# A hybrid attention and convolution block on one core: how the down projection's plain weights and its y tiles are brought in

## The chip, the core and the metric

The kernel runs on one core of a Trainium2 chip. A core has a matmul engine (TensorE, PE in the profile), three engines that work on tiles (VectorE is DVE, ScalarE is ACT, GpSimd is POOL), a sync engine (SP) and DMA queues that SP, ACT and POOL issue to. An engine takes its instructions in the order in which they stand in its queue; an instruction that waits holds up all behind it. The metric is the device time of one execution in microseconds. The inputs are float32, one sequence of 512 tokens of width 2048.

## The reference

One layer: a mixer (neighbourhood attention beside a conformer convolution, gated and merged) and then a feed-forward block, each behind an RMS norm and added to the stream. What the change touches is the end of the second:

```python
h = h + rms_norm(swiglu(rms_norm(h, ffn_pre_g)) @ w_down, ffn_post_g)
# swiglu(u): silu(u @ w_gate) * (u @ w_up), of width 5632
# rms_norm(y, g): y * rsqrt(mean(y * y) + 1e-6) * g
```

The down projection takes 5632 = 44 x 128 activations to 2048 = 16 x 128 outputs, for 512 tokens.

## The kernel before

Everything is held transposed: a tile is 128 features by 512 tokens. Float32 products are made from split operands: `x` is cast to `xh` (the name of the type is fp32r) on ACT, and DVE makes `xl = x - xh`; a product is then three matmuls, hi x lo, hi x hi and lo x hi. For most of the work Strassen-like products take fewer matmuls (`strassen`); what is left are plain tiles.

The down projection runs over 44 tiles of activations in five stages:

- *First plain stage*, `products_and_operands(0, 0, False)`: activations 0 to 3 against all 16 outputs. Each output `o` takes 12 matmuls of 512 columns into `pd0_o`. Its weights, 128 x 512, are loaded on SP's queue (`raw_wd`), cast on ACT (`whi_wd`, L134) and subtracted on DVE (`wlo_wd`, L135). ACT then copies the result to a tile `yf` of three buffers (L897) and stores it in `y_d` in DRAM from its own queue (L901). After every second output `prepare` makes operands for the next stage: loads `da` on GpSimd's queue, sums `dt` on DVE (L203 to L206), casts on ACT (L157) and subtractions on DVE (L158).
- *First Strassen stage*, `pairs(0, ...)`: 16 activation tiles by seven products for each two outputs. The results `ys` are multiplied by a row on GpSimd and accumulated into `y_d` by GpSimd's DMA (`added`, L912 and L913).
- *Second plain stage*, `products_and_operands(1, 36, True)`: activations 36 to 39. It is as the first, except that `yf` is accumulated into `y_d` by GpSimd's DMA (L899).
- *Second Strassen stage*, `pairs(1, ...)`.
- *Last part*: activations 40 to 43. `half(0)` does 256 of the 512 tokens for all outputs, two outputs in one bank `pl`, and `half(1)` the others. In the first half `weights(o)` loads and splits the weights of two outputs (`wl`, L144) and loads their `y` from `y_d` on SP's queue. When a bank is full, DVE adds `y` (L981), ACT squares the sum (`ysq`, L982), DVE sums the squares (L992, L994, and L988 for the last pair). The column sums of the squares (`r_s`), their power on GpSimd (`r_r`) and its spread over the partitions (`r_b`) give the norm's factor. The first half's outputs are finished during the second half (L1018, L1022); the second half's behind its end: a multiplication `yg` on DVE (L1031), an addition of `hb` (L1034, three on GpSimd and five on DVE) and the store.

The order on each engine is made by a scheduler from the program's order and its estimates; `keep_in_program_order` fixes an instruction in its place. Tiles of 128 x 512 come from 66 buffers (`slot`), weights in the rough from five (`raw`), split weights of the plain stages from three each (`whi`, `wlo`), PSUM has four `bank` and four `abank`.

Of the kernel before, what the change touches and what calls it, by code (L numbers as in the profile page):

```python
# [27 lines left out]
AF = mybir.ActivationFunctionType  # L28
# [3 lines left out]
P = 128  # L32
# [30 lines left out]
EARLY = 3  # L63
UN_EARLY, YA_EARLY = 2, 3
# [5 lines left out]
def hybrid_block(ctx: ExitStack, tc, xT, vecs, rpb, mask, w_c0, w_qk, w_v, w_gg, w_cg, w_ao, w_co, w_out, w_g0, w_gu, w_dn, outT):  # L70
# [795 lines left out]


    def products_and_operands(n, k0, add):
# [23 lines left out]
        added()  # L892
        for o in range(KT):
            ps = (bank, abank)[o % 2](f"pd{n}_{o}")
            gemm([(ps, w_dn[o, :, k0 * P : (k0 + DN_P) * P])], acts, f"wd{n}_{o}", n=DN_P, pin=o < 2)
# [40 lines left out]
    acts.extend([load(DN_3 + k) for k in range(EARLY, DN_P)])  # L936
    added()
    ha = []
# [9 lines left out]
    w, y, yg, r4 = [], [], [], []  # L948

    def weights(o):  # L950

        raw = wraw(f"wl{o}").rearrange("p (n k) -> p n k", n=2)
        nc.sync.dma_start(raw, w_dn[o : o + 2, :, DN_3 * P :].rearrange("n p k -> p n k"))
        for i in range(2):
            w.append(split(raw[:, i], f"wl{o + i}"))
            y.append(slot(f"y{o + i}"))
            load_in_order(y[o + i], y_d[o + i])

    def half(n, between={}):

        cols, other = ((A, B), (B, A))[n]
        acc = None
        for o in range(0, KT, 2):
            if n == 0:
                weights(o)
            ps = (bank, abank)[o // 2 % 2](f"pl{n}_{o}")
            sq = slot(f"ysq{n}_{o}")
            for i, part in enumerate((other, cols)):
                hi, lo = w[o + i]
                for k in range(DN_P):  # L970
                    s = slice(k * P, (k + 1) * P)
                    ah, al = (t[:, cols] for t in acts[k])
                    for wt, t in ((hi, al), (hi, ah), (lo, ah)):
                        nc.tensor.matmul(
                            ps[:, part], wt[:, s], t, start=k == 0 and t is al, stop=k == DN_P - 1 and wt is lo,
                            skip_group_check=True,
                        )
            between.get(o, lambda: None)()
            for i, part in enumerate((other, cols)):
                t = y[o + i][:, cols]  # L980
                nc.vector.tensor_tensor(out=t, in0=ps[:, part], in1=t, op=ALU.add)  # L981
                nc.scalar.activation(sq[:, part], t, AF.Square)  # L982
# [4 lines left out]
                if o == KT - 2 and i == 0:  # L987
                    nc.vector.tensor_tensor(out=acc[:, cols], in0=acc[:, cols], in1=sq[:, other], op=ALU.add)  # L988
            if acc is None:
                acc = sq  # L990
            elif o < KT - 2:
                nc.vector.tensor_tensor(out=acc, in0=acc, in1=sq, op=ALU.add)  # L992
# [129 lines left out]
```

## Time and profile before

| what | us |
|---|---|
| median of 3 runs | 2573.63 (2569.06 to 2574.58) |
| the profiled execution | 2566.05 |
| its span in the trace | 2564.3 |
| PE busy | 2509.8 |
| DVE busy | 2010.9 |
| ACT busy | 1196.8 |
| POOL busy | 466.9 |
| first plain stage begins | 2056.87 |
| second plain stage begins | 2265.82 |
| last part begins | 2476.34 |

The profile is of one execution. Its rows give the start in us from the span's start, the busy time, the engine, the line, the operation and what it makes from what, then partitions x elements; "x8" means that eight like instructions are put together. In brackets stands how long the engine sat idle before, and what ended that. "PEclk" is the clock that PE was granted, as a share of full speed. A matmul's busy time overlaps that of the next, so the pace of matmuls is read from their starts. A row with "q" behind an engine's name is of its DMA queue.

### The profile page before, as it was taken

Reading aid. Unit: us, or ns where it says so; the run is one execution under the profiler, and the core shown is the slowest. Engines: PE = TensorE matmul, PEld = TensorE weight load, DVE = VectorE, ACT = ScalarE, POOL = GpSimd, SP = SyncE. Lnnn points to the kernel's source line nnn. Section 1 sums busy time; section 2 is a strip of 40 time slices with the busy share of each in tenths; the row PEclk is TensorE's granted clock in tenths of the full one; section 3 lists DMA queues with packets and bytes.
Section 4 is the critical chain, followed back from the end, with each engine's and each line's share of the span. In section 5 each row is a group of like instructions: output and inputs, shape, how many; then the busy total and the mean of one; then the engine's idle time right before and its main releaser. Section 6 shows DMA issues by size and latency. Waiting matters only on the chain. (4 is left out here: it accounts for less than half of the span.)

```text
span 2564.3 us, 35709 instructions
## 1 busy us (share of the span) xinstructions
PE 2509.8 (98%) x13407; PEld 2165.6 (84%) x13407; DVE 2010.9 (78%) x2602; ACT 1196.8 (47%) x1838; POOL 466.9 (18%) x504
## 2 busy tenths in 40 slices
PE   9999999999999999999999999999999999999986
PEld 8888888878888888888988888888888878878876
DVE  5999896677776654338898888899987889888866
ACT  5223333455555422225455555555555564465433
POOL 0110222210000021001101111222222125442332
PEclk9999999999999999999999999999999999999988
DMA  6246323576667445337255566667666678888772
GB/s 209 94 145 197 109 93 108 160 244 184 183 194 250 141 139 185 99 100 221 94 174 170 172 178 182 183 196 208 207 202 189 191 269 227 230 197 224 196 221 92
DMA packets 154636, 452.41 MB, mean 176 GB/s; under 512 B 18144, under 2 KB 25440, under 8 KB 154464
## 3 DMA queue, kind: packets, MB, share of 16 engines
q1 hardware_dynamic: 103456, 324.32, 37.6%
q0 software_dynamic: 30336, 90.20, 16.7%
q10 hardware_dynamic: 20672, 35.63, 3.8%
q8 instruction: 105, 1.72, 0.3%
q14 instruction: 67, 0.55, 0.1%
HBM read 381.39 MB, written 61.87 MB: 173 GB/s over the span
## 5 line engine op out<-in xcount | busy, mean ns | idle before, releaser
L410 DVE SCALAR_TENSOR_TENSOR cv<-z,vec,cv 128x497 f32<-128x497 f32 (+14 forms) x240 | 190.9, 797 | 4.8
L135 DVE TENSOR_TENSOR wlo_wo<-raw_wo,whi_wo 128x1024 fp32r<-128x1024 f32 x36 | 47.5, 1318 | 106.6 <-ACT whi_wo L134 106.1
L800 POOL TENSOR_TENSOR row<-row,asq 128x512 f32<-128x512 f32 x30 | 41.1, 1370 | 414.3 <-ACT asq L799 414.3
L134 ACT CAST whi_wo<-raw_wo 128x1024 fp32r<-128x1024 f32 x36 | 37.9, 1053 | 130.0 <-PE po L184 122.7
L912 POOL TENSOR_TENSOR ys<-ys,row 128x512 f32<-128x512 f32 x32 | 55.6, 1739 | 138.0 <-DVE ys L302 83.8
L134 ACT CAST whi_y<-raw_y 128x1024 fp32r<-128x1024 f32 x32 | 33.5, 1052 | 79.0 <-PE py L184 75.7
L134 ACT CAST whi_qk<-raw_qk 128x1024 fp32r<-128x1024 f32 x32 | 33.6, 1051 | 77.2 <-PE qk L184 56.5
L135 DVE TENSOR_TENSOR wlo_qk<-raw_qk,whi_qk 128x1024 fp32r<-128x1024 f32 x32 | 40.3, 1259 | 32.3 <-ACT whi_qk L134 32.1
L827 POOL TENSOR_TENSOR an<-an,row 128x512 f32<-128x512 f32 x32 | 51.2, 1603 | 69.2 <-DMA an<-a_d 45.7
L667 DVE TENSOR_TENSOR gg<-py,gg 128x512 f32<-128x512 f32 x32 | 21.8, 689 | 52.2 <-PE py L185 52.2
L135 DVE TENSOR_TENSOR wlo_y<-raw_y,whi_y 128x1024 fp32r<-128x1024 f32 x32 | 53.3, 1667 | 10.9 <-ACT whi_y L134 10.4
L322 POOL TENSOR_TENSOR r_r<-r_v,mhalf 128x2 f32<-128x2 f32 (+1 forms) x6 | 7.0, 1172 | 292.1 <-DVE r_v L320 241.8
L181 PE MATMUL py<-ycl,whi_y 128*128 128x512 f32 x128 | 49.8, 389 | 0.0
L184 PE MATMUL py<-ych,whi_y 128*128 128x512 f32 x128 | 49.8, 389 | 0.0
L185 PE MATMUL py<-ych,wlo_y 128*128 128x512 f32 x128 | 49.8, 389 | 0.0
L860 ACT ACTIVATE sg<-sg 128x512 f32<-128x512 f32 x39 | 24.7, 634 | 51.2 <-DVE sg L302 51.2
L491 POOL TENSOR_TENSOR bm<-braw,msk 128x128 f32<-128x128 f32 x56 | 41.3, 770 | 16.2 <-DMA braw<-in_rpb 16.2
L677 POOL TENSOR_TENSOR gg<-gg,gg 128x512 f32<-128x512 f32 x16 | 20.6, 1288 | 112.2 <-ACT whi_y L134 70.8
L418 POOL TENSOR_TENSOR csum<-csum,cv 128x512 f32<-128x512 f32 x7 | 12.7, 1820 | 144.4 <-DVE cv L410 144.4
L163 PE MATMUL f<-b,whi_f 128*128 128x256 f32 x128 | 36.5, 285 | 0.8 <-DVE b L158 0.8
L164 PE MATMUL f<-b,whi_f 128*128 128x256 f32 x128 | 36.3, 283 | 0.0
L165 PE MATMUL f<-b,wlo_f 128*128 128x256 f32 x128 | 36.3, 283 | 0.0
(3195 smaller groups left out, 8778.0 us busy)
## 6 DMA issues: line engine op xcount, KB each, us to landing
raw_wo<-in_w_out SPq DMA_DIRECT2D x36, 512.0 KB, 3.8
raw_qk<-in_w_qk SPq DMA_DIRECT2D x32, 512.0 KB, 3.8
a_d<-sg ACTq DMA_DIRECT2D x44, 256.0 KB, 3.7
raw_v<-in_w_v SPq DMA_DIRECT2D x16, 512.0 KB, 4.4
raw_y<-in_w_ao SPq DMA_DIRECT2D x16, 512.0 KB, 3.7
gg<-g_d SPq DMA_DIRECT2D x32, 256.0 KB, 4.4
raw_y<-in_w_co SPq DMA_DIRECT2D x16, 512.0 KB, 3.6
raw_f<-in_w_g SPq DMA_DIRECT2D x16, 512.0 KB, 3.4
```

The costliest lines, as they stand in the source:

```text
L134: cast(hi[:, s], raw[:, s])
L135: nc.vector.tensor_tensor(out=lo[:, s], in0=raw[:, s], in1=hi[:, s].bitcast(F32), op=ALU.subtract)
L163: nc.tensor.matmul(o, hi, t[:, B], start=first, stop=False, skip_group_check=True)
L164: nc.tensor.matmul(o, hi, t[:, A], start=False, stop=False, skip_group_check=True)
L181: mmul = nc.tensor.matmul(ps, hi[:, s], al, start=first, stop=False)
L184: nc.tensor.matmul(ps, hi[:, s], ah, start=False, stop=False)
L185: nc.tensor.matmul(ps, lo[:, s], ah, start=False, stop=last)
L410: nc.vector.scalar_tensor_tensor(out=a[:, to], in0=z[:, fr], scalar=col(C_WDW, i * CW + w), in1=a[:, to], op0=ALU.mult, op1=ALU.add)
L491: nc.gpsimd.tensor_tensor(out=bm[:, o + i - i0], in0=raw[:, :, i * BC : (i + 1) * BC], in1=msk[:, o + i - i0, None, :].broadcast_to([P, RO ...
L800: nc.gpsimd.tensor_tensor(out=row[n], in0=row[n], in1=sq, op=ALU.add)
L827: nc.gpsimd.tensor_tensor(out=t, in0=t, in1=row[k // KT], op=ALU.mult)
L912: tc.keep_in_program_order(nc.gpsimd.tensor_tensor(out=t, in0=t, in1=row[n], op=ALU.mult))
```

## The change

In both plain stages the weights of two outputs are loaded at once (`loaded`), cast in one instruction of 128 x 1024 and subtracted in one, and this stands in the program one pair ahead of the pair that uses it. `four` issues a tile's 12 matmuls. In the last part the weights of six outputs are issued ahead of the first, and each turn issues those six ahead (`kept`, `AHEAD`). The loads of `y` move from SP's queue to GpSimd's, 14 of them ahead of the last two accumulations and two behind these. The last pair's squares get a tile each and go to the column sums as they are, without DVE's addition (L988), so that these take six matmuls and not four. Of the eight last additions of `hb` four, not three, are GpSimd's.

```diff
--- before.py
+++ after.py
@@ -61,6 +61,7 @@
 S1_AT = 3
 SPLIT = 2
 EARLY = 3
+AHEAD = 6
 UN_EARLY, YA_EARLY = 2, 3
 C_PRE, C_POST, C_FPRE, C_FPOST, C_LNG, C_LNB, C_BDW, C_WDW = 0, 16, 32, 48, 64, 72, 80, 88
 C_N = C_WDW + CT * CW
@@ -864,6 +865,30 @@
         activated(j, t)
     left = list(range(FT - DN_A[0] - KT - 2, 2 * KT))
 
+    def loaded(o, k0):
+
+        raw = wraw(f"w{k0}_{o}")
+        nc.sync.dma_start(
+            raw.rearrange("p (n k) -> p n k", n=2), w_dn[o : o + 2, :, k0 * P : (k0 + DN_P) * P].rearrange("n p k -> p n k")
+        )
+        return raw
+
+    def weights(o, k0):
+        raw = loaded(o, k0)
+        return wchunk(raw, f"wd{k0}_{o}", raw=raw)
+
+    def four(ps, hi, lo, cols, pin=False):
+
+        for k in range(DN_P):
+            s = slice(k * P, (k + 1) * P)
+            ah, al = (t[:, cols] for t in acts[k])
+            for i, (wt, t) in enumerate(((hi, al), (hi, ah), (lo, ah))):
+                mmul = nc.tensor.matmul(
+                    ps, wt[:, s], t, start=k + i == 0, stop=k + i == DN_P + 1, skip_group_check=True
+                )
+                if pin and k + i == 0:
+                    tc.keep_in_program_order(mmul)
+
 
     def products_and_operands(n, k0, add):
 
@@ -890,9 +915,13 @@
         for c in range(2):
             load_rows(c)
         added()
+        w = [weights(0, k0)]
         for o in range(KT):
             ps = (bank, abank)[o % 2](f"pd{n}_{o}")
-            gemm([(ps, w_dn[o, :, k0 * P : (k0 + DN_P) * P])], acts, f"wd{n}_{o}", n=DN_P, pin=o < 2)
+            if o % 2 == 0 and o + 2 < KT:
+                w.append(weights(o + 2, k0))
+            hi, lo = (t[:, o % 2 * NT : (o % 2 + 1) * NT] for t in w[o // 2])
+            four(ps, hi, lo, slice(0, NT), pin=o < 2)
             t = stp.tile([P, NT], F32, tag="quad", name=f"yf{o}", bufs=3)
             nc.scalar.copy(t, ps)
             if add:
@@ -934,7 +963,12 @@
 
 
     acts.extend([load(DN_3 + k) for k in range(EARLY, DN_P)])
+    y = [slot(f"y{o}") for o in range(KT)]
+    for o in range(KT - 2):
+        tc.keep_in_program_order(nc.gpsimd.dma_start(y[o], y_d[o]))
     added()
+    for o in (KT - 2, KT - 1):
+        tc.keep_in_program_order(nc.gpsimd.dma_start(y[o], y_d[o]))
     ha = []
     for i in range(0, KT - 4, 4):
         t = stp.tile([P, 4, HN], F32, tag="S" if i else "S1", name=f"ha{i}")
@@ -945,54 +979,43 @@
         tc.keep_in_program_order(nc.gpsimd.dma_start(t, h_d[i : i + 2, :, A].rearrange("k p t -> p k t")))
         ha.extend((t[:, 0], t[:, 1]))
 
-    w, y, yg, r4 = [], [], [], []
-
-    def weights(o):
-
-        raw = wraw(f"wl{o}").rearrange("p (n k) -> p n k", n=2)
-        nc.sync.dma_start(raw, w_dn[o : o + 2, :, DN_3 * P :].rearrange("n p k -> p n k"))
-        for i in range(2):
-            w.append(split(raw[:, i], f"wl{o + i}"))
-            y.append(slot(f"y{o + i}"))
-            load_in_order(y[o + i], y_d[o + i])
+    w, yg, r4 = [], [], []
+
+    def kept(o):
+
+        raw = loaded(o, DN_3)
+        w.extend(split(raw[:, i * NT : (i + 1) * NT], f"wl{o + i}") for i in range(2))
 
     def half(n, between={}):
 
         cols, other = ((A, B), (B, A))[n]
-        acc = None
+        acc, last = None, []
+        if n == 0:
+            for o in range(0, AHEAD, 2):
+                kept(o)
         for o in range(0, KT, 2):
-            if n == 0:
-                weights(o)
+            if n == 0 and o + AHEAD < KT:
+                kept(o + AHEAD)
             ps = (bank, abank)[o // 2 % 2](f"pl{n}_{o}")
-            sq = slot(f"ysq{n}_{o}")
             for i, part in enumerate((other, cols)):
-                hi, lo = w[o + i]
-                for k in range(DN_P):
-                    s = slice(k * P, (k + 1) * P)
-                    ah, al = (t[:, cols] for t in acts[k])
-                    for wt, t in ((hi, al), (hi, ah), (lo, ah)):
-                        nc.tensor.matmul(
-                            ps[:, part], wt[:, s], t, start=k == 0 and t is al, stop=k == DN_P - 1 and wt is lo,
-                            skip_group_check=True,
-                        )
+                four(ps[:, part], *w[o + i], cols)
             between.get(o, lambda: None)()
+            sq = [slot(f"ysq{n}_{o}")] * 2 if o < KT - 2 else [slot(f"ysq{n}_{o + i}") for i in range(2)]
             for i, part in enumerate((other, cols)):
                 t = y[o + i][:, cols]
                 nc.vector.tensor_tensor(out=t, in0=ps[:, part], in1=t, op=ALU.add)
-                nc.scalar.activation(sq[:, part], t, AF.Square)
+                nc.scalar.activation(sq[i][:, part if o < KT - 2 else cols], t, AF.Square)
                 if n:
                     if (o + i) % 4 == 0:
                         yg.append(wp.tile([P, 4, HN], F32, tag="raw", name=f"yg{o}", bufs=5))
                     nc.scalar.activation(yg[-1][:, (o + i) % 4], t, AF.Copy, scale=col(C_FPOST, o + i))
-                if o == KT - 2 and i == 0:
-                    nc.vector.tensor_tensor(out=acc[:, cols], in0=acc[:, cols], in1=sq[:, other], op=ALU.add)
-            if acc is None:
-                acc = sq
+            if o == 0:
+                acc = sq[0]
             elif o < KT - 2:
-                nc.vector.tensor_tensor(out=acc, in0=acc, in1=sq, op=ALU.add)
+                nc.vector.tensor_tensor(out=acc, in0=acc, in1=sq[0], op=ALU.add)
             if o == KT - 4:
                 nc.vector.tensor_tensor(out=acc[:, cols], in0=acc[:, cols], in1=acc[:, other], op=ALU.add)
-        return acc, sq
+        return acc, *sq
 
     def halved(n, squares, pin=False):
 
@@ -1030,7 +1053,7 @@
         t = yg[g]
         nc.vector.tensor_tensor(out=t, in0=t, in1=rb, op=ALU.mult)
         for m in range(0, 4, 2):
-            e = nc.gpsimd if g == 0 or g == 2 and m == 0 else nc.vector
+            e = nc.gpsimd if g == 0 or g < 3 and m else nc.vector
             e.tensor_tensor(out=t[:, m : m + 2], in0=t[:, m : m + 2], in1=hb[g][:, m : m + 2], op=ALU.add)
             q = nc.scalar if m else nc.sync
             q.dma_start(ov[4 * g + m : 4 * g + m + 2, :, B].rearrange("k p t -> p k t"), t[:, m : m + 2])
```

ACT's queue in the first plain stage, where the copy of tile 3 stands (`yf3`; `pd0_3` is its bank, `d..._` are operands for the Strassen stage). Before, with the cast of tile 4 behind the copy:

```order
L897 COPY yf3_18534<-pd0_3_18515 128x512
L134 CAST whi_wd0_4_0_0_18539<-raw_wd0_4_0_0_18538 128x512
L901 DMA y_d_11000<-yf3_18534 128x512
L157 CAST d11_2_18563<-da2_0_18411 128x256
L157 CAST d22_0_18566<-da2_1_18412 128x256
L157 CAST d22_1_18569<-da2_1_18412 128x256
L157 CAST d122_0_18577<-dt2_18572 128x256
L157 CAST d122_1_18580<-dt2_18572 128x256
L157 CAST d342_0_18583<-dt2_18572 128x256
L157 CAST d342_1_18586<-dt2_18572 128x256
L134 CAST whi_wd0_5_0_0_18591<-raw_wd0_5_0_0_18590 128x512
L134 CAST whi_wd0_6_0_0_18613<-raw_wd0_6_0_0_18612 128x512
```

The same place after the change, where the pairs 0, 2 and 4 are cast ahead of `yf0`:

```order
L926 COPY yf3_18528<-pd0_3_18515 128x512
L135 CAST whi_wd0_6_18534<-raw_w0_6_18532 128x1024
L930 DMA y_d_11000<-yf3_18528 128x512
L926 COPY yf4_18550<-pd0_4_18531 128x512
L158 CAST d11_2_18557<-da2_0_18417 128x256
```

The weights of tiles 4 and 5 no longer stand behind `yf3`; those of 6 and 7 do.

ACT's queue at the end of the second plain stage (`d1_0h` are casts for the first Strassen products: `q` for the first of them, `s2` for the second, `s1` for the third). Before:

```order
L259 CAST d1_0h_21121<-d1_0q_21113 128x1024
L897 COPY yf13_21034<-pd1_13_21015 128x512
L157 CAST d347_1_21082<-dt7_21068 128x256
L897 COPY yf14_21056<-pd1_14_21037 128x512
L259 CAST d1_0h_21145<-d1_0s2_21141 128x1024
L259 CAST d1_0h_21165<-d1_0s1_21110 128x1024
L897 COPY yf15_21104<-pd1_15_21085 128x512
L259 CAST d1_0h_21190<-d1_0s3_21188 128x1024
```

After the change:

```order
L158 CAST d347_0_20989<-dt7_20978 128x256
L926 COPY yf14_20966<-pd1_14_20953 128x512
L158 CAST d347_1_20992<-dt7_20978 128x256
L926 COPY yf15_21008<-pd1_15_20995 128x512
L260 CAST d1_0h_21049<-d1_0s2_21045 128x1024
L260 CAST d1_0h_21069<-d1_0s1_21014 128x1024
```

The casts of `s2` and `s1` stood between the copies of tiles 14 and 15 and now stand behind both.

ACT's queue at the start of the last part (`wl4h` is the cast of output 4's weights, `ysq0_0` the squares of outputs 0 and 1). Before:

```order
L144 CAST fa43h_22595<-ad43_22593 128x512
L144 CAST wl0h_22615<-raw_wl0_22613 128x512
L144 CAST wl1h_22621<-raw_wl0_22613 128x512
L982 ACTIVATE ysq0_0_22628<-y0_22619 128x256
L144 CAST wl2h_22659<-raw_wl2_22657 128x512
L982 ACTIVATE ysq0_0_22628<-y1_22625 128x256
L144 CAST wl3h_22665<-raw_wl2_22657 128x512
L982 ACTIVATE ysq0_2_22672<-y2_22663 128x256
```

After the change:

```order
L145 CAST fa43h_22499<-ad43_22497 128x512
L145 CAST wl0h_22551<-raw_w40_0_22549 128x512
L145 CAST wl1h_22555<-raw_w40_0_22549 128x512
L145 CAST wl2h_22561<-raw_w40_2_22559 128x512
L145 CAST wl3h_22565<-raw_w40_2_22559 128x512
L145 CAST wl4h_22571<-raw_w40_4_22569 128x512
L145 CAST wl5h_22575<-raw_w40_4_22569 128x512
L145 CAST wl6h_22581<-raw_w40_6_22579 128x512
L145 CAST wl7h_22585<-raw_w40_6_22579 128x512
L1007 ACTIVATE ysq0_0_22614<-y0_22503 128x256
L145 CAST wl8h_22621<-raw_w40_8_22619 128x512
```

The casts of outputs 2 to 7 stood behind squares and now stand ahead of all of them. In DVE's queue the subtractions move with their casts.

## The prediction

> **What bounds the kernel now.** I read first the page's line of busy times, then the windows by stage, and then the timeline of the matmul engine (PE) around its gaps, with what ended each. Times are us from the span's start.
>
> ```profile
> PE 2509.8 (98%) x13407; PEld 2165.6 (84%) x13407; DVE 2010.9 (78%) x2602; ACT 1196.8 (47%) x1838; POOL 466.9 (18%) x504
> ...
> core 0: us, PE busy (x) PEld busy (x) DVE busy (x) ACT busy (x) POOL busy (x), PEclk, DMA share, GB/s
> 2060.00:2115.00 55.00, 50.36 (x216) 40.67 (x215) 49.94 (x110) 39.45 (x91) 9.12 (x14) 0.94 0.77 270
> 2115.00:2262.00 147.00, 147.00 (x845) 129.46 (x844) 131.69 (x131) 73.82 (x101) 69.95 (x68) 1.00 0.82 220
> 2262.00:2330.00 68.00, 62.52 (x287) 51.22 (x286) 56.77 (x119) 44.54 (x101) 26.03 (x33) 0.95 0.89 235
> ...
> 2470.00:2510.00 40.00, 27.23 (x151) 24.27 (x149) 15.88 (x30) 10.70 (x25) 8.03 (x9) 0.83 0.83 274
> ```
>
> PE is busy 98% of the span, and all of it in the Strassen stages (second window: 147.00 of 147.00 at clock 1.00). The change touches the stages where PE is not full: the two plain stages (50.36 of 55 and 62.52 of 68) and the last part (27.23 of 40, clock 0.83). What ends the gaps there, as the rows below show, is a cast of weights (tiles whi_wd, wl). So I price each stage by the end of its PE work; the next one starts there.
>
> **First plain stage.**
>
> ```profile
> 2056.87 0.40 PE L181 MATMUL pd<-fa0l,whi_wd 128*128 128x512 f32 x1
> ...
> 2070.96 0.50 PE L181 MATMUL pd<-fa0l,whi_wd 128*128 128x512 f32 x1 [3.02 <-ACT whi_wd L134]
> ...
> 2105.87 0.39 PE L181 MATMUL pd<-fa0l,whi_wd 128*128 128x512 f32 x1
> ...
> 2108.36 0.39 PE L185 MATMUL pd<-fa3h,wlo_wd 128*128 128x512 f32 x1
> ...
> 2069.80 0.58 ACT L897 COPY yf<-pd 128x512 f32<-128x512 f32 x1 [0.81 <-DMA y_d<-yf]
> 2070.28 0.62 ACT L134 CAST whi_wd<-raw_wd 128x512 fp32r<-128x512 f32 x1
> ...
> 2074.00:2076.00 2.00, 2.00 (x6) 1.63 (x5) 2.00 (x7) 1.00 (x4) 0.00 (x0) 0.50 0.45 132
> ```
>
> The last tile's first and last matmuls are 2105.87 and 2108.36, 11 steps of 0.226. A tile of 12 is 2.72, 16 tiles 43.5. The stage lasts 2108.36 + 0.23 − 2056.87 = 51.7, so 8.2 are lost. The loss begins with the fourth yf copy (2069.80), which waits until an earlier yf has landed (three buffers); the weight cast stands behind it in ACT's queue (2070.28) and PE sits 3.02. Then the clock falls to 0.50 (window 2074 to 2076).
>
> ```profile
> L134 ACT CAST whi_wo<-raw_wo 128x1024 fp32r<-128x1024 f32 x36 | 37.9, 1053 | 130.0 <-PE po L184 122.7
> L135 DVE TENSOR_TENSOR wlo_qk<-raw_qk,whi_qk 128x1024 fp32r<-128x1024 f32 x32 | 40.3, 1259 | 32.3 <-ACT whi_qk L134 32.1
> ...
> L134 ACT CAST whi_wd<-raw_wd x32: 604/622/627, 2050.5 to 2310.7; 128x512 fp32r<-128x512 f32 x32
> L135 DVE TENSOR_TENSOR wlo_wd<-raw_wd,whi_wd x32: 678/686/694, 2052.7 to 2313.6; 128x512 fp32r<-128x512 f32 x32
> ```
>
> Two outputs now take one cast of 1.05 and one subtraction of 1.26, against 2 × 0.62 = 1.24 and 2 × 0.69 = 1.37. Over 16 pairs in both stages that is 16 × 0.19 = 3.0 us of ACT and 16 × 0.11 = 1.8 of DVE, beside PE: worth nothing by itself. What counts is the order. Pairs 0, 2 and 4 are cast ahead; pair 6 stands behind the yf copy of tile 3. Cast 2070.28 + 1.05 = 2071.3, subtraction by about 2072.7; PE wants it at 2056.87 + 6 × 2.72 = 2073.2. So the wait goes, with a margin of about 0.5. What is late next is the stage's end: in the new ACT order the last yf copy stands ahead of the first cast that the following product needs, which I put at 2 us of PE waiting (a DVE chain of some 1.2 plus a cast of 1.05). **Gain 8.2 − 2 = 6.2**; bounds 0, if a cast still lands behind a late copy, and 8.2.
>
> **Second plain stage.** Its yf tiles are accumulated into y_d by GpSimd's DMA.
>
> ```profile
> 2265.82 0.48 PE L181 MATMUL pd<-fa36l,whi_wd 128*128 128x512 f32 x1
> ...
> 2289.98 0.79 PE L181 MATMUL pd<-fa36l,whi_wd 128*128 128x512 f32 x1 [2.83 <-ACT whi_wd L134]
> ...
> 2318.28 1.98 PE L264 MATMUL d<-d,d_0h 128*128 128x512 f32 x8
> ...
> 2321.05 2.00 PE L264 MATMUL d<-d,d_0h 128*128 128x512 f32 x8
> ...
> 2277.32 0.59 ACT L897 COPY yf<-pd 128x512 f32<-128x512 f32 x1
> 2288.82 0.58 ACT L897 COPY yf<-pd 128x512 f32<-128x512 f32 x1
> ...
> 2317.23 0.59 ACT L897 COPY yf<-pd 128x512 f32<-128x512 f32 x1 [1.54 <-DMA y_d<-yf]
> ...
> 2309.22 0.87 POOL L899 DMA_DIRECT2D y_d<-yf  x1 [2.15 <-ACT d L157]
> ```
>
> It lasts 2318.28 − 2265.82 = 52.5 against 43.5, a loss of 9.0 of the same kind (2.83 at 2289.98). With weights by pairs PE would be through the tiles at 2265.82 + 43.5 = 2309.3. But the copies can't follow. An accumulation issued at 2309.22 releases the copy at 2317.23, 8.0 later; with 0.85 from copy to issue, three copies (there are three yf buffers) take about 8.9, where PE needs 3 × 2.72 = 8.2 and is already ahead. Tile 3's copy stays at 2277.32 and tile 6's at about 2288.8, since operand casts and landings set these. Three hops more are 2288.8 + 3 × 8.9 = 2315.5, and with about 1 for operand casts in between tile 15 is copied at 2316.5. The casts for the second Strassen product now stand behind this copy: 0.6 + 1.05 gives its start at 2318.1, against 2321.05 before. PE idles on the way, and a half-clock stretch like that of the first stage costs some 1.5. **Gain 3.0 − 1.5 = 1.5.** By a landing time of 7 it is some 3, by 9 nothing, and 9.0 if copies hold up nobody; below nothing see the fourth rival.
>
> **Last part.**
>
> ```profile
> 2476.34 0.39 PE L974 MATMUL pl<-fa40l,wl0h 128*128 128x256 f32 x1 [1.50 <-ACT wl0h L144]
> ...
> 2482.13 0.28 PE L974 MATMUL pl<-fa43h,wl1l 128*128 128x256 f32 x1
> ...
> 2508.24 0.76 DVE L981 TENSOR_TENSOR y<-pl,y 128x256 f32<-128x256 f32 x2 [1.79 <-PE pl L974]
> ...
> 2508.70 0.42 ACT L982 ACTIVATE ysq<-y 128x256 f32<-128x256 f32 x1 [3.35 <-DVE y L981]
> 2509.03 0.60 ACT L144 CAST wl10h<-raw_wl 128x512 fp32r<-128x512 f32 x1
> ...
> 2509.68 0.39 PE L974 MATMUL pl<-fa40l,wl10h 128*128 128x256 f32 x1 [1.47 <-ACT wl10h L144]
> 2514.78 0.39 PE L974 MATMUL pl<-fa40l,wl12h 128*128 128x256 f32 x1 [1.47 <-ACT wl12h L144]
> ...
> 2489.83 0.42 DVE L981 TENSOR_TENSOR y<-pl,y 128x256 f32<-128x256 f32 x1 [4.39 <-DMA y<-y_d]
> ...
> 2543.76 0.28 PE L974 MATMUL pl<-fa40l,wl15h 128*128 128x256 f32 x1
> ...
> 2545.08 0.28 PE L974 MATMUL pl<-fa43h,wl15l 128*128 128x256 f32 x1
> ```
>
> A pair of outputs takes 2514.78 − 2509.68 = 5.10 in the first half. Its 24 matmuls at 0.12 (2543.76 to 2545.08 is 11 steps) are 2.88. The rest is a ring: PE ends, DVE adds y (2508.24), ACT squares it (2508.70), only then casts the next weights (2509.03), and PE starts at 2509.68. Twice DVE also waits for a y load (4.39). Now weights for four pairs are cast before the first square, so the ring is cut. The first pair is as before (its casts wait for the same weights and for fa43): it ends at 2482.13 + 0.12 = 2482.25. Seven pairs at 2.88 end the first half at 2502.4. For the second half I take 25.4: 16 × 12 × 0.12 = 23.0, some 0.8 for the first half's column sums and their spread, and 1.6 for banks that DVE frees late; the halves overlap before, so no row shows it alone. PE ends at 2527.8, against 2545.08 + 0.28 = 2545.36. **Gain 17.6.** ACT has 16 casts of 0.60 and 16 squares of 0.42, 16.3 of 26; DVE 11 (casts) + 6 (y) + 5 (sums) = 22 of 26: both fit. Bounds: 10 if the loads or DVE hold half of it back, 18.5 if the second half too runs at 23.0 plus its sums.
>
> The y loads leave SP's queue and go to GpSimd's:
>
> ```profile
> 2473.00 1.28 POOL L912 TENSOR_TENSOR ys<-ys,row 128x512 f32<-128x512 f32 x1 [11.11 <-DVE ys L302]
> ...
> 2053.10 3.70 POOL L875 DMA_DIRECT2D da<-as_d  x7
> ...
> y_d<-yf POOLq DMA_DIRECT2D x16, 256.0 KB, 7.1
> ```
>
> GpSimd idles 11.11 ahead of 2473.00. A load is issued in 3.70 / 7 = 0.53, so 14 take 7.4 and are hidden. The last two follow the two remaining accumulations (issued near 2477, landing 8 later) and are wanted only near 2500. In SP's queue only weight loads are left, which is why the first ones need not be late. Behind the y loads in GpSimd's queue stand the ys multiplications and the ha loads, used from 2531: no price.
>
> **Tail.**
>
> ```profile
> 2548.30 1.05 PE L312 MATMUL r_s<-ones,ysq 128*128 128x1 f32 x8 [2.94 <-DVE ysq L988]
> ...
> 2559.47 1.29 DVE L1034 TENSOR_TENSOR yg<-yg,hb 128x512 f32<-128x512 f32 x2
> ```
>
> One DVE addition of the last squares goes (the two small matmuls more cost little), worth up to 0.5. One of DVE's five final additions, 1.29 / 2 = 0.65, goes to GpSimd, beside DVE's others. **Gain 1.0**, bounds 0 and 1.4.
>
> **Sum.** 6.2 + 1.5 + 17.6 + 1.0 = 26.3. The profiled execution took 2566.05 (span 2564.3), so it becomes 2539.7. The median of the runs is 2573.63, 7.6 above the profiled one; the same 26.3 taken from it and rounded gives **2547**.
>
> **A rule against the change.** The Trainium skill, "DMA: Bandwidth & Descriptors", section "SWDGE vs HWDGE vs iDMA", says that DMAs issued from GpSimd have their descriptors written by that engine into SBUF state that DVE shuts it out of in its two-port mode, and that those of SP and ACT are immune. By it the y loads could be issued late while DVE works. The row at 2053.10 shows seven issues at 0.53; no run here shows 14 beside a Strassen stage. The sum, by 0.53, stands without this at 2547; by the rule the third rival's 2557 is nearer.
>
> **Rivals.**
> - *Plain tiles wholly free* (0.17). The accumulations land faster than their copies need. Against it: the 8.0 above. Gains 8.2 + 8.0 + 17.6 = 33.8: 2540.
> - *Plain tiles give nothing* (0.15). The cast of pair 6 or 8 still waits behind a copy; margin 0.5 only. Then 17.6 + 1.0 = 18.6: 2555.
> - *y loads late* (0.07). If an issue in GpSimd's queue takes 1.55, not 0.53, the 14 last 21.7 from 2462 and push the last two multiplications, their accumulations and so the last two y loads past 2502. Half of the last part's gain is lost: 6.2 + 1.5 + 9 = 16.7, 2557.
> - *Slower* (0.03). The change makes copies, not weights, the limit of the second plain stage. If a landing takes L, four hops of L + 0.85 run from 2277.3, and the second product starts 2.65 behind the last; at L = 15.6 that is 24.8 later than before and eats up 6.2 + 17.6 + 1.0; at 17 it is 30.3 later, and with 1.5 for the clock the kernel is at 2580. Against it: 8.0 in the row above, and the median of 7.1 over the sixteen.
> - *The order changes nothing* (0.03). Were the weights' landing and not their cast the limit, PE would wait as long for the pairs; only the tail's 1.0 is left: 2573. Against it: no wait quoted here ends with a weight's DMA.
>
> **How the numbers follow.** The forecast has 0.55. Low end: plain tiles free and the last part at its upper bound, 8.2 + 9.0 + 18.5 + 1.4 = 37.1, to 2536. High end: the third rival's 2557 and the 4.6 by which the runs shown differ from their median (2569.06 and 2573.63), to 2562. That leaves out less than 2 in 10. A measurement of this kernel tells about 0.2% (5 us) from no change. Faster by over that 0.94, within it 0.03, slower 0.03.
>
> **What would show it.** Right: in the first plain stage no PE wait for whi over 1 us; in the second a PE gap of 5 us or more after the last plain tile with ACT's yf copies waiting for y_d<-yf; in the last part 2.88 a pair at clock 1.00 from the second pair on; 14 y loads within 10 us on GpSimd before 2473. Wrong: DVE waiting for y, PE still pacing at 5.1, or the second plain stage ending later than 2321.

## The result and the profile after

| | before | after |
|---|---|---|
| median, us | 2571.78 (4 runs, 2569.06 to 2574.58) | 2543.65 (4 runs, 2541.38 to 2544.70) |
| ratio | 1 | 0.9889, 95% interval 0.9872 to 0.9906 |
| profiled execution | 2566.05 | 2541.38 |
| its span | 2564.3 | 2539.6 |

The kernel is 28.1 us faster between the medians and 24.7 between the two profiled executions, each at least as fast as every run shown here of its kernel. The forecast of the median was 2547. The rows that answer to those of before, from the page, the windows and the timelines of the changed kernel (the helper lines are one further down):

```profile
PE 2499.8 (98%) x13415; PEld 2158.5 (85%) x13415; DVE 2004.1 (79%) x2583; ACT 1194.1 (47%) x1822; POOL 477.4 (19%) x521
...
core 0: us, PE busy (x) PEld busy (x) DVE busy (x) ACT busy (x) POOL busy (x), PEclk, DMA share, GB/s
2056.00:2099.00 43.00, 43.00 (x191) 35.59 (x190) 38.09 (x92) 30.71 (x76) 6.56 (x13) 1.00 0.81 285
2099.00:2107.00 8.00, 5.51 (x21) 4.02 (x20) 7.96 (x11) 6.13 (x11) 3.14 (x4) 0.79 0.64 210
2262.00:2306.00 44.00, 42.94 (x188) 34.81 (x188) 33.24 (x85) 29.09 (x71) 21.37 (x28) 1.00 0.94 234
2306.00:2318.00 12.00, 8.52 (x37) 6.80 (x36) 11.02 (x19) 7.77 (x15) 2.62 (x3) 0.86 0.91 156
2470.00:2510.00 40.00, 37.28 (x305) 36.67 (x306) 26.93 (x53) 18.85 (x44) 9.72 (x14) 1.00 0.57 187
```

The plain tiles now run without a gap in the first stage (43.00 of 43.00) and with one of 1.06 in the second (42.94 of 44.00; a wait for DVE's wlo_wd), both at clock 1.00. The loss has moved into the first microseconds of the Strassen stages (5.51 of 8, 8.52 of 12, at clocks 0.79 and 0.86). In the last part PE is at 37.28 of 40, against 27.23. Where the first plain stage hands over:

```profile
2099.12 0.39 PE L886 MATMUL pd<-fa3h,wlo_wd 128*128 128x512 f32 x1
2101.99 3.64 PE L265 MATMUL d<-d,d_0h 128*128 128x512 f32 x8 [2.48 <-ACT d_0h L260]
2105.52 1.21 PE L267 MATMUL d<-d,d_0l 128*128 128x256 f32 x8
2106.56 2.00 PE L265 MATMUL d<-d,d_0h 128*128 128x512 f32 x8
```

PE waits 2.48, and then the eight matmuls of the product take 3.64 where the next eight of that shape take 2.00: the clock has fallen (it was granted at 0.50 from 2102 to 2105). At the end of the second plain stage, PE first, then ACT and DVE:

```profile
2306.87 1.98 PE L265 MATMUL d<-d,d_0h 128*128 128x512 f32 x8
2311.33 1.22 PE L267 MATMUL d<-d,d_0l 128*128 128x256 f32 x8 [2.49 <-DVE d_0l L262]
2313.55 3.68 PE L265 MATMUL d<-d,d_0h 128*128 128x512 f32 x8 [0.99 <-ACT d_0h L260]
...
2303.70 0.59 ACT L926 COPY yf<-pd 128x512 f32<-128x512 f32 x1 [1.37 <-DMA y_d<-yf]
...
2309.59 0.59 ACT L926 COPY yf<-pd 128x512 f32<-128x512 f32 x1
...
2304.62 0.43 DVE L159 TENSOR_TENSOR d<-dt,d 128x256 fp32r<-128x256 f32 x1 [0.89 <-ACT d L158]
...
2310.06 1.22 DVE L262 TENSOR_TENSOR d_0l<-d_0q,d_0h 128x1024 fp32r<-128x1024 f32 x1
2311.20 1.22 DVE L250 TENSOR_TENSOR d_0s<-d_0s,d_0q 128x1024 f32<-128x1024 f32 x1
```

The tiles end at 2306.87, where the first product starts; the second starts at 2313.55. In the stage's second half only one landing is late (the copy at 2303.70, 1.37), and it costs DVE 0.89; the copies at 2282.06 and 2283.35 had waited 4.76 and 0.71 for landings, and PE did not stop there. What ends last is DVE's queue: the last operands, then d_0l at 2310.06, d_0s at 2311.20. The last copy (2309.59) is done 2.27 before ACT's cast of d_0s can start (2312.45). And the last part:

```profile
2470.50 0.39 PE L886 MATMUL pl<-fa40l,wl0h 128*128 128x256 f32 x1 [1.50 <-ACT wl0h L145]
...
2472.57 0.39 PE L886 MATMUL pl<-fa40h,wl0l 128*128 128x256 f32 x1 [1.56 <-DVE wl0l L145]
...
2475.18 0.28 PE L886 MATMUL pl<-fa43h,wl1l 128*128 128x256 f32 x1
...
2478.06 0.28 PE L886 MATMUL pl<-fa43h,wl3l 128*128 128x256 f32 x1
...
2493.18 0.39 PE L886 MATMUL pl<-fa40l,wl14h 128*128 128x256 f32 x1 [0.43 <-ACT wl14h L145]
...
2521.33 0.28 PE L886 MATMUL pl<-fa43h,wl15l 128*128 128x256 f32 x1
2522.98 0.61 PE L313 MATMUL r_s<-ones,ysq 128*128 128x1 f32 x4 [1.37 <-DVE ysq L1017]
```

A pair takes 2478.06 − 2475.18 = 2.88, and behind the first pair only the waits at output 14 are left, 0.43 for its cast and 0.23 for its subtraction.

The account by stages, which is used for every run below: *first* runs from the first plain stage's first matmul to the second's, *second* from there to the last part's first matmul, *last* to the end of its last matmul, *tail* to the span's end.

| kernel | median | first | second | last | tail | sum |
|---|---|---|---|---|---|---|
| before | 2571.8 | 208.95 | 210.52 | 69.02 | 18.94 | 507.43 |
| after | 2543.7 | 205.72 | 208.98 | 51.11 | 17.99 | 483.80 |
| plain_alone | 2565.9 | 205.65 | 206.21 | 73.18 | 18.83 | 503.87 |
| last_alone | 2551.8 | 209.21 | 210.60 | 52.89 | 18.28 | 490.98 |
| no_ahead | 2563.2 | 205.65 | 209.94 | 67.63 | 18.56 | 501.78 |
| y_on_sp | 2552.4 | 205.67 | 209.93 | 58.47 | 19.61 | 493.68 |
| y_sp_early | 2556.2 | 205.65 | 209.22 | 59.45 | 20.20 | 494.52 |
| y_pool_late | 2543.3 | 205.95 | 208.14 | 51.29 | 18.15 | 483.53 |
| y_on_sp_ha_last | 2547.5 | 205.65 | 208.56 | 50.53 | 19.26 | 484.00 |
| ahead2 | 2544.8 | 205.64 | 208.87 | 52.17 | 18.42 | 485.10 |
| head | 2543.1 | 204.36 | 208.96 | 52.72 | 18.04 | 484.08 |
| wl0_early | 2541.6 | 205.64 | 206.45 | 51.52 | 17.93 | 481.54 |
| tail_old | 2544.7 | 205.94 | 207.67 | 51.49 | 19.36 | 484.46 |
| best3 | 2540.3 | 204.40 | 207.29 | 48.93 | 17.96 | 478.58 |

Ahead of the first plain stage all of them do the same work, but for the loads and casts of its first weights, and yet it starts anywhere from 2055.80 to 2061.30. So spans are not compared below, but stages, and medians where they say enough. Each stage's figure is of one profiled execution. How far such figures scatter, the table shows itself: the second stage takes 206.2 to 209.9 in kernels whose plain tiles and Strassen products are the same there, and the last part 51.1 to 52.9 in five that differ there by no more than the moment of the y loads or the last squares (`after`, `tail_old`, `y_pool_late`, `head`, `last_alone`).

### The profile page after: what moved, and what is told of

Read it like the earlier page. It is cut to its first block, busy times and chain, and to the rows that moved or that the text cites. A ratio compares the mean times of both kernels' runs of the same rounds, so it can differ in the third digit from the quotient of the medians.

```text
span 2539.6 us, 35631 instructions
## 1 busy us (share of the span) xinstructions
PE 2499.8 (98%) x13415; PEld 2158.5 (85%) x13415; DVE 2004.1 (79%) x2583; ACT 1194.1 (47%) x1822; POOL 477.4 (19%) x521
## 4 chain that ended last, share of the span: by engine, by line
PE 85%; DVE 8%; issue 3%; DMA 2%; ACT 1%; POOL 1%; ACTq 0%; DVEq 0%; POOLq 0%; SPq 0%
PE f L265 20%; PE f L267 10%; PE d L265 8%; PE g L265 7%; PE d L267 4%; PE g L267 4%; PE qk L186 2%; PE qk L185 2%; PE qk L182 2%; PE po L185 2%; PE po L186 2%; PE po L182 2%; PE py L182 2%; PE py L186 2%; PE py L185 2%
## 5 line engine op out<-in xcount | busy, mean ns | idle before, releaser
L861 ACT ACTIVATE sg<-sg 128x512 f32<-128x512 f32 x39 | 24.7, 634 | 50.2 <-DVE sg L303 50.2
```

## The experiments

**Do the stages add up?** `plain_alone` is the kernel before with the plain tiles' edit only:

```diff
-            gemm([(ps, w_dn[o, :, k0 * P : (k0 + DN_P) * P])], acts, f"wd{n}_{o}", n=DN_P, pin=o < 2)
+            if o % 2 == 0 and o + 2 < KT:
+                w.append(weights(o + 2, k0))
+            hi, lo = (t[:, o % 2 * NT : (o % 2 + 1) * NT] for t in w[o // 2])
+            four(ps, hi, lo, slice(0, NT), pin=o < 2)
```

> The kernel before with the weights of the plain tiles taken two at a time, and nothing else of the change. If the stages are priced rightly by the two traces, the start of the second plain stage comes about 3 us earlier and that of the last part about 5 us earlier than in the kernel before, the last part keeps its 69 us, and the time falls by 4 to 6 us. The rival, that the difference between the two traces in the plain stages is scatter between executions (1.1 us of it arises before the first changed instruction), gives less than 2 us.

2565.9 us, ratio 0.9979 (0.9968 to 0.9989): about 5 us, as expected in sum but not in its parts. The first stage gains 3.30, as in the changed kernel. But the second gains 4.31 there and 1.54 in the changed kernel, with the same edit, and the last part is 4.16 longer than before, not the same: here too DVE waits for y, 5.23 and 1.40, and PE 4.55 for wl4h behind it.

`last_alone` is the changed kernel with the lines above turned round, the plain tiles as before.

> The kernel before with all of the change but the plain tiles' pairs. If the stages add up, 19 us of the change are here (17.9 up to the last matmul, 1.0 behind it): 17 to 21 us faster than before, with the last part at 51 us and both plain stages as before, their waits for whi_wd of about 3 us included. If the earlier end of the plain stages helps the last part (by weights or y tiles that are then in place), this gives less than 15 us.

2551.8 us, ratio 0.9920 (0.9904 to 0.9937), 19 us below the median of before in its runs (2570.9): as expected. The last part takes 52.89 (51 was expected), the plain stages are as before. The two alone sum to 5 + 19 = 24 by the medians, of the 28; by the ratios it is 0.0021 + 0.0080 against 0.0111, which the intervals don't tell apart.

**The ring or the y loads?** `no_ahead` keeps the y loads on GpSimd and takes the early casts away:

```diff
-AHEAD = 6
+AHEAD = 0
```

> The changed kernel with the last part's weights issued by pairs as before (AHEAD 0), y loads in GpSimd's queue. If the ring was the cost, the first half's pairs are back at 5.1 us each and this loses about 15 us against the changed kernel: 8 pairs at 5.1 against 2.9, less the overlap of the last two with the second half. If the y loads carried it, it loses less than 7 us.

`y_on_sp` keeps the early casts and puts the y loads back, behind their weights:

```diff
-    for o in range(KT - 2):
-        tc.keep_in_program_order(nc.gpsimd.dma_start(y[o], y_d[o]))
...
+        for i in range(2):
+            y.append(slot(f"y{o + i}"))
+            load_in_order(y[o + i], y_d[o + i])
```

> The changed kernel with the y loads back in SP's queue, two behind each weight load as before. If the ring through the casts was the cost, the early casts alone cut it and this loses at most 1.5 us against the changed kernel. The rival, that the late y loads carried a good part, lets DVE wait for y again as before (4.4 and 1.6 us) and loses 5 to 7 us.

Of the 17.9 us that the last part gains, the move of the y loads alone gives 1.4 (69.02 to 67.63) and the early casts alone 10.6 (to 58.47); the rest needs both. Without the casts the last part is 16.5 longer than the changed kernel's, where about 15 was expected, and PE's timeline shows the ring at its old pace, 2504.13 − 2499.03 = 5.10:

```profile
2499.03 0.39 PE L886 MATMUL pl<-fa40l,wl8h 128*128 128x256 f32 x1 [1.53 <-ACT wl8h L145]
...
2504.13 0.38 PE L886 MATMUL pl<-fa40l,wl10h 128*128 128x256 f32 x1 [1.47 <-ACT wl10h L145]
```

With the casts but y on SP there is one long stall, which DVE passes on to PE (`y_on_sp`, DVE, then PE, then the landing times of its y loads):

```profile
2487.15 0.42 DVE L1004 TENSOR_TENSOR y<-pl,y 128x256 f32<-128x256 f32 x1 [6.65 <-DMA y<-y_d]
2488.65 0.68 DVE L145 TENSOR_TENSOR wl6l<-raw_w,wl6h 128x512 fp32r<-128x512 f32 x1
...
2489.39 0.58 PE L886 MATMUL pl<-fa40h,wl6l 128*128 128x256 f32 x1 [4.89 <-DVE wl6l L145]
...
DMA to landing us min/median/max: 5.9/7.1/13.2
```

The subtraction for wl6 stands behind the y addition in DVE's queue. So the expectation that the casts alone would do was wrong, and the rival, which said 5 to 7 us, was nearer: the last part is 7.4 longer than the changed kernel's.

What made y late, the moment, the queue, or something beside it? `y_sp_early` puts the loads of the changed kernel's place in SP's queue, `y_pool_late` puts all sixteen behind the last accumulations in GpSimd's:

```diff
-        tc.keep_in_program_order(nc.gpsimd.dma_start(y[o], y_d[o]))
+        load_in_order(y[o], y_d[o])
```

> The changed kernel with the y loads at the place in the program that it gives them, but in SP's queue. In the run with the y loads back by pairs the last part lost 7.4 us up to its last matmul, DVE waiting 6.7 us for a y tile while the DMA engines were at a share of 1.03. If the moment of the loads is what counts (14 of them ahead of the last product's end, when the DMA engines have room), this is within 2 us of the changed kernel in the last part. If it is the queue (GpSimd's beside SP's), the last part is again 5 us or more longer.

```diff
-    for o in range(KT - 2):
-        tc.keep_in_program_order(nc.gpsimd.dma_start(y[o], y_d[o]))
     added()
-    for o in (KT - 2, KT - 1):
+    for o in range(KT):
         tc.keep_in_program_order(nc.gpsimd.dma_start(y[o], y_d[o]))
```

> The changed kernel with all sixteen y loads in GpSimd's queue but behind the last two accumulations, not 14 of them ahead. If the moment of the loads counts, since the DMA engines are full (share 1.0) from the last product's end on, DVE waits for y again and the last part is 5 to 9 us longer than the changed kernel's. If it is enough that they are out of SP's queue, where the weight and hb loads stand, the last part is within 2 us.

`y_sp_early` did not put the loads early: on SP they stood behind the hb loads and were issued from 2470.80. It loses 8.3 in the last part, but by another wait, since the weights of outputs 10 and 11 now stand behind sixteen y loads (its PE):

```profile
2498.77 0.58 PE L886 MATMUL pl<-fa40l,wl10h 128*128 128x256 f32 x1 [7.76 <-ACT wl10h L145]
```

`y_pool_late` issued its y loads from 2473.97 to 2488.60, beginning 1.6 us behind the last part's first matmul, where the changed kernel begins 14.5 ahead of it. DVE waited 1.29 and 1.44 for y, and the last part lost nothing: 51.29. So it is not the moment. Either SP's queue is the cost, or the loads of `ha` (the part of `h` that is added to the first half's outputs in the end; 2 MB): in GpSimd's queue they stand behind y both here and in the changed kernel, while with y on SP they ran beside it. `y_on_sp_ha_last` is `y_on_sp` with the ha loads behind all y loads, in SP's queue as well:

```diff
-        tc.keep_in_program_order(nc.gpsimd.dma_start(t, h_d[i : i + 4, :, A].rearrange("k p t -> p k t")))
...
     s1, s2 = halved(0, half(0), pin=True)
+    ha = []
...
+        load_in_order(t, h_d[i : i + 4, :, A].rearrange("k p t -> p k t"))
```

> The run with the y loads back in SP's queue by pairs, but with the five ha loads (2 MB, used 25 us later) taken out of GpSimd's queue and put behind all y loads in SP's. With y in GpSimd's queue the ha loads stand behind y at either place tried, and the last part keeps its 51 us; with y in SP's queue they ran beside y, whose landing took up to 13.2 us. If the ha loads' share of the DMA engines is what made y late, the last part is back within 3 us of the changed kernel's (51.1 us). If it is SP's own queue (hb and weights ahead of y in it), it stays 5 us or more longer, as the 58.5 us of the run before.

The last part takes 50.53 with every y load in SP's queue. DVE still waits for y, but never more than 2.56:

```profile
2484.88 0.42 DVE L994 TENSOR_TENSOR y<-pl,y 128x256 f32<-128x256 f32 x1 [2.56 <-DMA y<-y_d]
```

The DMA engines are full either way. The column ahead of the last is their share, first of `y_on_sp`, then of `y_on_sp_ha_last`, each around its longest wait for y; the slowest landing of a y tile falls from 13.2 to 7.4 at most.

```profile
2480.00:2488.00 8.00, 4.49 (x38) 4.29 (x36) 0.92 (x2) 1.17 (x3) 0.00 (x0) 0.97 1.02 358
```

```profile
2483.00:2491.00 8.00, 7.76 (x65) 7.56 (x64) 4.62 (x10) 3.98 (x9) 0.00 (x0) 1.00 1.05 388
```

So what the move of the y loads brought is that the ha loads, which nobody needs for 25 us, went behind them. The queue that carries y is not the cause, and neither is the moment within 16 us. (The Trainium skill, "DMA: Bandwidth & Descriptors", section "Issuing engines are not separate DMA queues", says the same: all issuing engines' transfers share the same 16 DMA engines and interleave there. The two last parts, 50.53 and 58.47 with one queue for y, agree.) The profiled execution of `y_on_sp_ha_last` starts the first plain stage at 2061.30, and its tail is 1.3 longer than the changed kernel's; the tails of all three kernels with y on SP are 1.3 to 2.2 longer. No run looked for why.

**How far ahead?** `ahead2` issues the weights two outputs ahead:

```diff
-AHEAD = 6
+AHEAD = 2
```

> The changed kernel with the last part's weights issued two outputs ahead and not six. A pair's casts then stand ahead of the squares of the pair before it, which is enough to cut the ring: by that theory the last part takes 51 to 53 us, within 2 us of the changed kernel. The rival, that six are needed since the weights land late behind other loads, gives a last part of 55 us or more, with PE waiting for wl.

52.17 us and a median of 2544.8: one pair of lead cuts the ring. The other two pairs bring 1 us by these two traces, which is no more than the 51.1 to 52.9 of kernels with the same last part; the medians differ by 1.2.

**What the first plain stage gives back.** `head` loads and casts the weights of the first product after each plain stage ahead of the last plain pair's tiles:

```diff
+            if o == KT - 2:
+                raw = wraw(f"head{n}")
+                nc.sync.dma_start(raw, w_dn[0, :, DN_A[n] * P : DN_A[n] * P + 1024])
+                heads.append((raw, wchunk(raw, f"head{n}", raw=raw)))
```

> The changed kernel with the weights of the first Strassen product after each plain stage loaded and cast ahead of the last plain tile. In the changed kernel PE waits 2.48 us there for this cast, which stands behind the last yf copy, and then runs the product at half the clock (3.64 us for 8 matmuls that take 1.98 elsewhere). If that place in ACT's queue is what gives back part of the first plain stage's gain, the span from the first plain stage's first matmul to the second's falls from 205.7 to 202 to 203.5 us and the time by 2 to 5 us. The rival, that DVE's operands for the product end the wait whatever stands in ACT's queue, gives less than 1 us. The second plain stage, where DVE's subtraction ends the wait, is expected to gain at most 1.5 us.

First: 204.36, a gain of 1.36, between the two theories. The product now follows the plain tiles at once and at full clock, but the second waits (its PE):

```profile
2102.17 1.98 PE L268 MATMUL d<-d,whi_head 128*128 128x512 f32 x8
2103.98 1.11 PE L270 MATMUL d<-d,wlo_head 128*128 128x256 f32 x8
2106.71 2.11 PE L268 MATMUL d<-d,d_0h 128*128 128x512 f32 x8 [1.62 <-ACT d_0h L263]
```

The order on ACT did cost the 2.48 and the half clock. Behind it stands the next cast, itself queued behind a copy of the first product. The medians (2543.1 and 2543.7) don't show the gain. In the second plain stage nothing is gained (208.96): the first product's wait for d_0l is gone, but PE waits 2.75 ahead of the second, for a cast of what DVE made last.

**The start of the last part.** `wl0_early` splits the weights of outputs 0 and 1 ahead of the last product's copies; `best3` does so for outputs 0 to 3 and the last activation tile, keeps `head`, and fixes the order of the subtractions and y additions on DVE:

```diff
             if o == KT - 4:
-                behind = early(k0)
+                acts_first = early(k0)
+                behind = (lambda: (acts_first(), kept(0))) if n else acts_first
```

> The changed kernel with the casts of the last part's first two weights ahead of the last Strassen product's copies. PE waits 1.50 us for the cast and 1.56 us for the subtraction there, both behind the last activation tile's (fa43). If these stand in each other's way only by the order, both waits go and the last part is 2 to 3 us shorter. The rival, that fa43 itself is late (PE needs it nine matmuls, about 1.1 us, after the start), leaves 1.5 us of the wait: a gain of 1 to 2 us.

```diff
+                behind = (lambda: (acts_first(), acts.append(load(DN_3 + EARLY)), kept(0), kept(2))) if n else acts_first
...
-                nc.vector.tensor_tensor(out=t, in0=ps[:, part], in1=t, op=ALU.add)
+                add = nc.vector.tensor_tensor(out=t, in0=ps[:, part], in1=t, op=ALU.add)
+                if n == 0:
+                    tc.keep_in_program_order(add)
```

> The changed kernel with the first Strassen weights of each plain stage cast ahead (as in the run on that), and with the last activation tile and the weights of outputs 0 to 3 split ahead of the last copies of the last Strassen product, in a fixed order on ACT and DVE. If the waits of the last part's start (1.50 and 1.56 us) are matters of order, both go: 2 to 4 us faster than the changed kernel, PE going from the last product into the last part with less than 0.5 us of wait. If the last activation's load is late, a wait of 1 to 2 us for fa43 stays and the gain is 1 to 2 us.

Since the last part now starts earlier than it can go on, the measure is from the last eight matmuls of the last product to the end of the last part: 53.72 in the changed kernel, 52.47 in `wl0_early` (waits of 1.79 for fa43l and 1.21 for wl2l remain, as the rival said), 49.89 in `best3`, where PE goes over without a wait:

```profile
2470.05 1.12 PE L270 MATMUL d<-d,d_14l 128*128 128x256 f32 x8
2471.01 0.28 PE L890 MATMUL pl<-fa40l,wl0h 128*128 128x256 f32 x1
```

So it was order, with fa43 too, worth 3.8 here. `best3` has a median of 2540.3, ratio 0.9880 (0.9866 to 0.9895): by the stages 5.2 us better than the changed kernel (1.7 of it in the second stage, which scatters by more), by the medians 3.4, by the ratios to before not told apart from its 0.9889 (0.9872 to 0.9906).

**The tail.** `tail_old` turns both edits of the tail back:

```diff
-            e = nc.gpsimd if g == 0 or g < 3 and m else nc.vector
+            e = nc.gpsimd if g == 0 or g == 2 and m == 0 else nc.vector
...
+                if o == KT - 2 and i == 0:
+                    nc.vector.tensor_tensor(out=acc[:, cols], in0=acc[:, cols], in1=sq[0][:, other], op=ALU.add)
```

> The changed kernel without its two edits of the tail: the last squares are again added on DVE and three, not four, of the last additions are GpSimd's. By the traces (18.94 us from the last matmul to the span's end before, 17.99 after) this costs 0.7 to 1.2 us there: 0.6 for the addition on DVE, the rest for the sums. A rival is that GpSimd's fourth addition, 1.4 us, ends as late as DVE's last, so that only the sums' 0.3 are left.

The tail is 19.36 against 17.99: 1.4, a little over the range. The first column sum waits 2.76 for DVE instead of 1.37, and the spread of the sums (`r_b`) starts 5.46 behind the last matmul instead of 4.50. So 0.96 is the squares' and sums' share, and 0.4 is left for GpSimd's fourth addition: the split expected was the other way round, and the rival's 0.3 is too little.

## Why the prediction was right, step by step

It said 26.3 us less for the profiled execution; that fell by 24.7, and 1.07 of this arises ahead of the first plain stage. The median fell by 28.1, 2573.63 having been the median of three runs and 2571.78 that of four, so how near 2547 came to 2543.65 says little about the terms. These are, from the prediction and from the stages:

| term | predicted | traces |
|---|---|---|
| first plain stage | 6.2 | 3.23 |
| second plain stage | 1.5 | 1.54 |
| last part | 17.6 | 17.91 |
| tail | 1.0 | 0.95 |

- *First plain stage.* The mechanism was right: the tiles run at 0.226 a matmul without a gap, the weights of pair 6 come in time, and what is late next is the first Strassen cast behind the last copy. The size was not. The step that failed is "which I put at 2 us of PE waiting": the wait was 2.48, and the half clock behind it, charged in the second plain stage and forgotten here, made eight matmuls 3.64 instead of 2.00. `head` shows both go with the order on ACT, though the next cast takes most of it back. The tiles themselves did gain the whole 8.2: they end 2099.35 − 2055.80 = 43.55 after their start instead of 51.7. Of this 5.0 was given back behind them: the 2.48, some 1.7 by the clock, and smaller pieces (a wait of 0.24 at 2112.55 among them).
- *Second plain stage.* The sum was right by luck, and its reason mostly wrong. The prediction let landings of y_d<-yf carry tile 15's copy to 2316.5 and the second product to 2318.1 with it. The stage began 4.30 earlier than before; put on the old clock, that copy came at 2313.9, 2.6 sooner than said, and the second product at 2317.85, as said, but behind something else. (The gap of 5 us or more with copies waiting for landings, named as a sign of being right, did not show: PE waited 2.49 and 0.99, for DVE's work.) The chain of waits over this stretch (start, duration, what) has one landing in it and then DVE's operands:

```profile
2295.90 7.70 DMA y_d<-yf
2303.70 0.59 ACT yf L926
...
2308.74 1.02 DVE d L159 x4
...
2311.20 1.23 DVE d_0s L250
2312.45 1.05 ACT d_0h L260
2313.55 3.68 PE d L265 x8
```

  The landing took 7.70, near the 8.0 assumed, but the hops did not add: copies of tiles 6 to 15 found their buffers free except this once, that of tile 12. What was missed is that DVE, ahead of whose queue PE now runs, sets the start; no run took work off DVE there, so this rests on the chain alone. The half clock cost 3.68 − 2.00 = 1.7, near the 1.5 assumed. `head` could not help here, as DVE's work stays. And with 206.2 to 209.9 for the same work in other kernels, one trace's 1.54 bears out no sum to a tenth.
- *Last part.* As worked out: 2.88 a pair, and the second half's first matmul at 2496.64, which is 26.14 after the start against 26.06. That it is so near is in part luck: the first pair took 4.80 and not 5.91, since the clock stayed up, and what the waits at output 14 cost made up for it. The second half took 2521.61 − 2496.64 = 24.97 and not 25.4. (The upper bound of 18.5 does not follow from its own terms: 23.0 and 0.8 for the sums would make it 19.2.) The 5.10 was read from the pairs late in the first half. The first three of before, from 2476.34 on, took more, 7.59, 7.33 and 8.23 from start to start, with waits for y and a low clock on top of the ring (granted 0.57 from 2484 to 2488 and 0.50 from 2492 to 2496), so that 5.10 is the least that a pair took and not the mean:

```profile
2483.93 0.39 PE L974 MATMUL pl<-fa40l,wl2h 128*128 128x256 f32 x1 [1.52 <-ACT wl2h L144]
2491.26 0.52 PE L974 MATMUL pl<-fa40l,wl4h 128*128 128x256 f32 x1 [2.27 <-ACT wl4h L144]
2499.49 0.38 PE L974 MATMUL pl<-fa40l,wl6h 128*128 128x256 f32 x1 [1.47 <-ACT wl6h L144]
```

  The parts of the explanation fared unevenly. The ring was shown (`no_ahead`: 16.5 us lost). For the y loads the prediction named the right worry, DVE waiting for y (in the changed kernel it waits for none), and the wrong cure: their room ahead of the last product is not needed (`y_pool_late`), nor GpSimd's queue (`y_on_sp_ha_last`); the 2 MB of ha that the move put behind them is. It was given no price ("no price" for the ha loads behind y), and with the early casts in place it decides 7.9 us (58.47 against 50.53).
- *The loads on GpSimd.* They did not take 7.4 us to issue: 

```profile
2456.01 3.75 POOL L968 DMA_DIRECT2D y<-y_d  x7
...
2466.96 0.54 POOL L968 DMA_DIRECT2D y<-y_d  x1 [0.97 <-DMA y<-y_d]
2467.51 1.30 POOL L941 TENSOR_TENSOR ys<-ys,row 128x512 f32<-128x512 f32 x1
```

  An issue is 0.54, as said, but seven go out at once, and from the eighth on GpSimd waits between issues (0.15 to 1.15), mostly for an earlier transfer to land. Whether the chip or the program's semaphores set this, no run shows. Fourteen fill 2456.01 to 2467.50, 11.5 us and not the 10 named as a sign; that is about all of the gap, 11.1 before, and the multiplication behind them starts at once. The rule of the Trainium skill ("DMA: Bandwidth & Descriptors", section "SWDGE vs HWDGE vs iDMA") that speaks against GpSimd's queue while DVE runs in its two-port mode shows no sign here: DVE was busy 7.44 of the 11 us from 2456 to 2467, and the issues stay at 0.54. In which mode DVE ran, the profile does not say, so the rule is not tested. The landings' median is 6.7, against 5.9 in the kernel before and 7.1 in `y_on_sp`, both in SP's queue.
- *Tail.* 0.95 of 1.0; undoing it costs 1.4, most of it by the sums, where the prediction gave them the smaller part.

## What to carry to other kernels

When a stage is freed of a wait, price what its successor needs first, and the clock that the new gap costs, before counting the whole of the old loss as gain. Where a cast for the next tile stands in an engine's queue behind work on this tile's result, one step of lead (here a pair of outputs) was enough to cut the ring; more lead bought 1 us at most. And when the DMA engines are full (a share of 1.02 and more here), moving a load is worth what it displaces: look for traffic that nobody waits for yet and put that last, in whichever queue.

## What the runs showed of the hardware

The same waits do not give the same clock. In the changed kernel PE waits 1.50 and 1.56 at the start of the last part, with two matmuls between, and runs on at 1.00 (the pair ends 4.8 us after its start). Waits of 1.50 and 1.43 in the kernel before, and of 1.50 and 2.08 in `last_alone`, are followed by half clock, and the pair takes 5.9 and 7.35. In `y_on_sp_ha_last` the waits are 1.50 and 1.43 again, as in the kernel before, and there the clock stays at 1.00 and the pair takes 4.65. After the gap at the second plain stage the half clock lasts under 4 us in the changed kernel and over 5 in `y_on_sp` (windows of the two, in this order; the column ahead of the DMA share is the clock):

```profile
2314.00:2316.00 2.00, 2.00 (x6) 1.52 (x6) 2.00 (x3) 1.87 (x3) 0.00 (x0) 0.50 0.82 154
2318.00:2320.00 2.00, 2.00 (x12) 1.66 (x11) 1.72 (x2) 0.90 (x2) 0.00 (x0) 1.00 0.90 291
```

```profile
2314.00:2316.00 2.00, 1.91 (x5) 1.54 (x6) 2.00 (x3) 2.00 (x4) 0.00 (x0) 0.50 0.92 131
2318.00:2320.00 2.00, 2.00 (x10) 1.90 (x10) 0.31 (x1) 0.95 (x1) 0.00 (x0) 0.50 0.97 320
```

The Trainium skill ("TensorE: Matmul & The Clock Gate", section "What's actually happening") says that the clock falls after at least one idle window of some 3.4 us, and that this window runs freely, so that a turn depends on where in it a change falls. By the first, the 2.48 alone should not have turned the clock, and here it did; the measurement decides. The second would give such differences, and perhaps some of the spread of the second stage, 206 to 210 us, among kernels that do the same there. No run here set a gap's place on purpose.
